# Score bursts of two pairs, an early Exp table, one maximum per head and a halved last output group in a two-layer encoder

## The chip, the cores and the metric

The kernel runs on one core of one Trainium2 chip. The metric is the device time of one execution in microseconds (us); lower is better. A core has five engines that run side by side and meet through semaphores: TensorE (PE in the profile; PEld are its weight loads), VectorE (DVE), ScalarE (ACT), GpSimd (POOL) and SyncE (SP), which issues most transfers. Matmul results land in PSUM, eight banks of 512 fp32 columns on 128 partitions.

## The reference, cut to what matters

Two layers of an encoder over 256 tokens of width 1024, in fp32. Each layer is a mixer and a channel sublayer:

```
h = rms_norm(x, n1);  proj = h @ w_in                  # 1024 -> 2560
a: 4 heads, neighbourhood attention with a bias        # q, k normed
d: 6 heads, dilated windows, q and k normed and rotated
c: 6 heads over 2 key heads, full attention, q and k normed and rotated
mix = [rms_norm(a), rms_norm(d), rms_norm(c)] * og;  x = x + mix @ w_out
h = rms_norm(x, n2);  g, u = split(h @ w_gate_up)      # 1024 -> 2 x 2816
g = conv3(g) + b;  x = x + (gelu(g) * u) @ w_down      # 2816 -> 1024
```

Every head's softmax is p = exp(s - max) / sum over 256 keys. With 256 tokens a head's scores are two token tiles of 128 rows and 256 columns, and one PSUM bank holds both.

## The kernel before, in words

**Arithmetic.** Each fp32 operand is split in a high part (a cast, on ScalarE) and a low part (operand minus high part, on VectorE), and a product is three matmuls: high x high, high x low, low x high (`mm3`, line 695). Weights arrive as raw tiles (4 buffers) through SyncE's queue and are split into hi and lo tiles (2 buffers of each) a unit at a time (`load`, `split`, `unit`, lines 640 to 693). Six units of layer 1's output projection are split while layer 0's feed-forward part runs, stored to DRAM (`keep`, line 624) and read back through GpSimd's queue.

**Stages of a layer.** Norm and transposes of x (`split_T`), projections into the four banks of the pool psa, then attention in the order d, c, a, with the projections and output projections woven in as filler (`Weave`), then `out_projections`, then the feed-forward part in eleven steps of 256 columns: gate G (`gate`, line 1373), U (`up`, line 1392), and down projection D (`down`, line 1402) in the order of `FFN` (line 77). The D of the last two steps come together, in four groups: two halves of 512 output columns by two token tiles. Lines 1437 to 1444 add each group to x on VectorE and, in the last layer, store it.

**Attention.** `scores(i)` (line 1210) computes two heads' scores in one burst of 12 matmuls of half height: the heads of a pair sit on partitions 0 to 63 and 64 to 127 and their matmuls run side by side. `softens` (line 1062) takes the row maximum (for d and a heads in one VectorE pass with the bias, for c heads by `reduce_max`), then Exp with its row sum on ScalarE, then the division. `turn` transposes the weights on TensorE and splits them, `weigh` multiplies them with the values. Scores, turned weights, transposed q and k, and the heads' outputs share the pool psw, four banks.

**Order.** All engines' order is planned before anything is emitted (`Plan`, line 238). Each operation has a rank, its number in program order plus shifts (`later`, `PLACES`). `order` (line 319) walks through time with a cost for each operation (`cost`, line 473) and always takes what can start earliest, lowest rank first. PSUM and SBUF buffers are given out strictly in program order of first use. A burst (`together`) runs without anything else between on TensorE, and starts only when all the buffers that it wants are free at once (`at_of_burst`, line 362). For transfers the planner books a rate and a latency (lines 436 to 448), and `LANDS` says when the thirteen first transfers land. The order is then fixed: on the chip each engine runs its list in order and waits by semaphore. `not_before(e)` makes an operation wait for the last one of engine e that was added so far.

The profile gives nearly every instruction line 470, where operations are emitted, so tiles tell them apart: `psw_w` and `psa_a` are the two PSUM pools, `wp_raw`, `wp_hi`, `wp_lo` weights, `act_ch` and `act_cl` the split turned weights in attention and the split product of gate and U in the feed-forward part, `act_s2k` scratch, `const_x` the running x, `small_nm` the negated maxima.

Of the kernel before, what the change touches and what calls it, by code (L numbers as in the profile page):

```python
# [11 lines left out]
F32 = mybir.dt.float32  # L12
# [6 lines left out]
P = 128  # L19
S = 256  # L20
# [31 lines left out]
LANDS = (4074, 3054, 5167, 3987, 5363, 6065, 7002, 7704, 8406, 9342, 10278, 10308, 10337)  # L52
# [172 lines left out]
def handover(a, b):  # L225
# [12 lines left out]
class Plan:  # L238
    def __init__(self, tc):
        self.tc, self.ops, self.shift, self.burst, self.bursts, self.behind = tc, [], 0, None, {}, None  # L240
        for name, short in (("tensor", "PE"), ("scalar", "ACT"), ("vector", "DVE"), ("gpsimd", "POOL"), ("sync", "SP")):
            setattr(self, name, PlanEngine(self, short, getattr(tc.nc, name)))
# [26 lines left out]
    def add(self, engine, method, args, kw):  # L269
# [16 lines left out]
        o.ns, o.lat, o.size, o.kind = cost(engine.name, method, args, kw, ins)  # L286
        o.before, o.after, o.first, o.tiles = set(), [], [], []
# [31 lines left out]
    def order(self):  # L319
# [79 lines left out]
        while len(done) < len(ops):  # L399
            best = None  # L400
            for e, r in ready.items():
                for i in r:
# [9 lines left out]
                    if at is not None and (best is None or (at, o.rank) < best[:2]):  # L412
                        best = (at, o.rank, i)
# [22 lines left out]
            if o.method == "dma_start":  # L436
# [6 lines left out]
                if e == "POOL":  # L443
                    end += 1000
                wires[ring] = end + shared / 120 + (o.size - shared) / (280 if i < self.first_loads else 335)
                end = wires[ring] + 1200
# [26 lines left out]
def cost(engine, method, args, kw, ins):  # L473

    out = args[0]
    if method == "dma_start":
# [3 lines left out]
        size = 4 * math.prod(w.shape) * (2 if small else 2 if spread else 1)  # L480
# [34 lines left out]
def encoder_kernel(  # L515
# [74 lines left out]
    nc.gpsimd.memset(minus_half, -0.5)  # L590

# [283 lines left out]
    for l in range(DEPTH):  # L875
# [181 lines left out]
        class Head:  # L1057
# [4 lines left out]
            def softens(self, sps):  # L1062
# [17 lines left out]
                else:  # L1080

                    for t in range(NT):
                        nc.vector.reduce_max(nm[:, t : t + 1], sps[t], axis=AX.X, negate=True)
# [125 lines left out]

        def scores(i):  # L1210

            two = heads[i : i + 2]
            sps = [psw.tile([P, NT, S], F32, tag="w", name=f"s_{z.name}") for z in two]
            g = two[0].group
            with nc.together():
                for t in range(NT):
                    for x, y in ((0, 0), (0, 1), (1, 0)):
                        for z, sp, rows_ in zip(two, sps, (LOW, HIGH)):
                            nc.tensor.matmul(
                                sp[:, t], turned[g + "q"][x][rows_, z.h // 2, t * P : (t + 1) * P],  # L1220
                                turned[g + "k"][y][rows_, z.kv if g == "c" else z.h // 2],
                                start=(x, y) == (0, 0), stop=(x, y) == (1, 0),
                            )
            for z, sp in zip(two, sps):
                z.softens([sp[:, t] for t in range(NT)])
# [147 lines left out]
        def gate(s):  # L1373
# [16 lines left out]
            made[s] = B  # L1390

# [10 lines left out]
        def down(steps):  # L1402
            ws = [unit() for _ in steps]
            for h in range(2):
                hs = slice(h * 512, (h + 1) * 512)
                for t in range(NT):
                    c = slice(t * P, (t + 1) * P)
                    for s, (wh, wl) in zip(steps, ws):
                        ch, cl = ready[s]
                        for j in range(2):  # L1410
                            mm3(
# [103 lines left out]
```

## Time and profile before

| | |
|---|---|
| median of three runs | 614.18 us (614.12 to 614.36) |
| profiled execution | 614.38 us, of which the span of instructions is 612.6 |
| TensorE busy | 604.5 us, 99% of the span, 3484 matmuls |
| VectorE, ScalarE busy | 485.4 us (79%), 428.5 us (70%) |
| GpSimd busy | 84.3 us (14%) |
| DMA | 121.44 MB, mean 198 GB/s |

A group row of the profile reads: line, engine, operation, out<-in, shapes, count, then busy us, mean ns of one, and the engine's idle time before it with what ended it. A timeline row reads: start in us, length in us, engine, instruction, and in brackets the idle time before it and its releaser. A row of a stretch reads: from:to, its length, then busy us with instruction counts in brackets for PE, PEld, DVE, ACT and POOL, the granted clock, the DMA engines' share and GB/s. Matmuls are pipelined: one's length reaches into the next, so what a matmul costs TensorE is the time from its start to the next one's.

### The profile page before, as it was taken

How to read it: one execution, taken by the hardware profiler on the slowest of the kernel's cores; microseconds unless marked ns; L12 is line 12 of the kernel's file. 1: busy time of each engine (PE TensorE's matmuls, PEld its weight loads, DVE VectorE, ACT ScalarE, POOL GpSimd, SP SyncE). 2: the span in 40 equal slices, each digit the busy share in tenths (PEclk: the TensorE clock that was granted, in tenths of full speed). 3: DMA queues.
4: the chain of work that ended last, by engine and by line, in shares of the span. 5: the costliest groups of instructions: out<-in, count | busy, mean ns of one | idle time of the engine just before them, and what ended most of it. 6: DMA issues, size and time to landing. Idle time of an engine off the chain costs nothing.

```text
span 612.6 us, 9883 instructions
## 1 busy us (share of the span) xinstructions
PE 604.5 (99%) x3484; PEld 525.2 (86%) x3484; DVE 485.4 (79%) x1000; ACT 428.5 (70%) x1064; POOL 84.3 (14%) x136
## 2 busy tenths in 40 slices
PE   8999999999999999999999999998999999999997
PEld 6998888888888888888899989887888888888885
DVE  4899989797788988887777788767877777777774
ACT  6789999696565766675588889857755656566661
POOL 2732130202400000000032214231000000000000
PEclk9999999999999999999999999999999999999999
DMA  8893403557589799987555626654665555556501
GB/s 272 294 294 141 139 25 105 184 159 242 166 225 326 247 360 326 349 293 251 155 155 182 215 70 240 206 178 129 202 217 179 175 197 201 167 185 205 189 18 68
DMA packets 85073, 121.44 MB, mean 198 GB/s; under 512 B 9864, under 2 KB 69608, under 8 KB 85024
## 3 DMA queue, kind: packets, MB, share of 16 engines
q1 hardware_dynamic: 82752, 112.17, 56.6%
q0 software_dynamic: 1728, 8.39, 4.0%
q8 instruction: 27, 0.44, 0.3%
q10 hardware_dynamic: 544, 0.26, 0.2%
q14 instruction: 22, 0.18, 0.1%
HBM read 110.93 MB, written 9.88 MB: 197 GB/s over the span
## 4 chain that ended last, share of the span: by engine, by line
PE 92%; DVE 2%; ACT 2%; POOL 1%; DMA 1%; issue 1%; SPq 0%; DVEq 0%; POOLq 0%
PE psw_w L470 51%; PE psa_a L470 41%; DMA const_x<-in_x_dram 1%; ACT act_s2k L470 1%; POOL small_rstd L470 1%; DVE const_x L470 1%; DVE wp_lo L470 1%; SPq L470 0%; DVE act_sw L470 0%; DVE act_z L470 0%; ACT wp_hi L470 0%; POOL small_ms L470 0%; ACT L470 0%; ACT act_z L470 0%; ACT act_hT L470 0%
## 5 line engine op out<-in xcount | busy, mean ns | idle before, releaser
L470 DVE TENSOR_TENSOR wp_lo<-wp_raw,wp_hi 128x512 fp32r<-128x512 f32 (+2 forms) x332 | 232.1, 735 | 53.9 <-ACT wp_hi L470 36.8
L470 ACT CAST wp_hi<-wp_raw 128x512 fp32r<-128x512 f32 (+2 forms) x332 | 202.5, 663 | 21.7 <-PE psa_a L470 9.1
L470 PE MATMUL psw_w<-act_hT,wp_hi 128*128 128x512 f32 x704 | 181.4, 393 | 0.0
L470 PEld LDWEIGHTS psw_w<-act_hT,wp_hi 128*128 128x128 f32 x704 | 128.1, 189 | 24.7
L470 PE MATMUL psa_a<-wp_hi,act_hT 128*128 128x384 f32 (+2 forms) x448 | 113.3, 332 | 0.5 <-ACT wp_hi L470 0.5
L470 PEld LDWEIGHTS psw_w<-act_hT,wp_lo 128*128 128x128 f32 x704 | 97.9, 190 | 6.9
L470 PE MATMUL psw_w<-act_hT,wp_lo 128*128 128x256 f32 x704 | 102.8, 282 | 0.0
L470 PEld LDWEIGHTS psa_a<-wp_hi,act_hT 128*128 128x128 f32 x448 | 78.1, 189 | 4.0 <-ACT wp_hi L470 0.8
L470 PE MATMUL psa_a<-wp_lo,act_hT 128*128 128x384 f32 (+2 forms) x224 | 74.2, 333 | 0.3 <-DVE wp_lo L470 0.2
L470 ACT COPY act_s2k<-psw_w 128x256 f32<-128x256 f32 x88 | 32.2, 371 | 58.7 <-PE psw_w L470 58.5
L470 PE MATMUL psa_a<-wp_lo,act_ch 128*128 128x512 f32 x176 | 69.4, 394 | 0.0
L470 PE MATMUL psa_a<-wp_hi,act_cl 128*128 128x512 f32 x176 | 69.4, 395 | 0.0
L470 PE MATMUL psa_a<-wp_hi,act_ch 128*128 128x512 f32 x176 | 68.9, 394 | 0.0
L470 DVE TENSOR_TENSOR act_s2k<-psw_w,act_s2k 128x256 f32<-128x256 f32 x88 | 36.7, 422 | 15.2 <-ACT act_s2k L470 14.9
L470 PEld LDWEIGHTS psa_a<-wp_lo,act_hT 128*128 128x128 f32 x224 | 42.2, 188 | 3.0 <-DVE wp_lo L470 1.7
L470 PEld LDWEIGHTS psa_a<-wp_hi,act_cl 128*128 128x128 f32 x176 | 33.2, 188 | 7.9 <-DVE act_cl L470 0.3
L470 PEld LDWEIGHTS psa_a<-wp_hi,act_ch 128*128 128x128 f32 x176 | 33.2, 189 | 6.7
L470 PEld LDWEIGHTS psa_a<-wp_lo,act_ch 128*128 128x128 f32 x176 | 33.1, 188 | 6.8
L470 DVE SCALAR_TENSOR_TENSOR act_s2k<-act_s2k,act_cw,act_s2k 128x255 f32<-128x255 f32 x88 | 36.8, 482 | 1.4 <-ACT act_s2k L470 1.3
L470 ACT ACTIVATE act_s2k<-act_s2k,act_cw 128x256 f32<-128x256 f32 x44 | 24.1, 595 | 18.0 <-DVE act_s2k L470 18.0
L470 ACT ACTIVATE act_s2k<-act_s2k 128x512 f32<-128x512 f32 x22 | 13.9, 631 | 30.0 <-DVE act_s2k L470 30.0
L470 POOL TENSOR_TENSOR small_rstd<-small_ms,const_mh 128x6 f32<-128x6 f32 (+2 forms) x26 | 31.7, 1218 | 2.2
(112 smaller groups left out, 794.7 us busy)
## 6 DMA issues: line engine op xcount, KB each, us to landing
wp_raw<-in_w_gate_up_dram SPq DMA_DIRECT2D x44, 1024.0 KB, 5.2
wp_raw<-in_w_down_dram SPq DMA_DIRECT2D x22, 1024.0 KB, 5.0
wp_raw<-in_w_in_dram SPq DMA_DIRECT2D x14, 768.0 KB, 6.3
wp_raw<-in_w_in_dram SPq DMA_DIRECT2D x8, 1024.0 KB, 8.8
wp_raw<-in_w_out_dram SPq DMA_DIRECT2D x8, 768.0 KB, 9.5
dram_khi<-act_mixT_hi SPq DMA_DIRECT2D x4, 768.0 KB, 9.5
dram_klo<-act_mixT_lo SPq DMA_DIRECT2D x4, 768.0 KB, 9.8
wp_lo<-dram_klo POOLq DMA_DIRECT2D x4, 768.0 KB, 5.4
```

The lines of the kernel that those rows point to most:

```text
L470: getattr(o.engine.real, o.method)(*map(real, o.args), **{k: real(v) for k, v in o.kw.items()})
```

## The change

- **Bursts.** `BURSTS` gives the number of pairs in a burst: heads d0 to d3 in one, d4 and d5 in one, c0 to c3, c4 and c5, a0 to a3. Each is one `together` over up to four score tiles; the softmax of the second pair is still added at its own place in the program.
- **Table.** Behind layer 0's last Gelu stands an Exp of one column into a new tile `few_out`, not before that Gelu in time. The planner's cost now has 1290 ns for each change between Exp and Gelu.
- **Maximum.** A c head's two token tiles have one `reduce_max` over the whole bank, two results wide.
- **Last group.** In the last layer, the down projection's last group (columns 512 to 1023 of the second token tile) is made in two halves of 256 columns, the second in a psw bank named `end`; each half has its own addition to x and its own store.
- **Planner.** Transfers: 360 bytes per ns in place of 335, 1000 ns latency in place of 1200, no further 1000 ns for GpSimd's queue, stores counted at 1.5 times their size; a tie goes to the lower number; new `LANDS` and `PLACES`. START and the warm-up, the order and number of first transfers, stay as they are.

```diff
--- before.py
+++ after.py
@@ -49,7 +49,7 @@
 ]
 
 
-LANDS = (4074, 3054, 5167, 3987, 5363, 6065, 7002, 7704, 8406, 9342, 10278, 10308, 10337)
+LANDS = (4100, 3300, 5300, 3450, 5800, 6450, 7250, 8200, 8900, 9800, 10700, 10750, 10800)
 
 
 WARM, WARM_MORE, WARM_W = 13, 15, 256
@@ -227,17 +227,18 @@
 
 
 PLACES = {
...
 }
 
 
 class Plan:
     def __init__(self, tc):
-        self.tc, self.ops, self.shift, self.burst, self.bursts, self.behind = tc, [], 0, None, {}, None
+        self.tc, self.ops, self.shift, self.burst, self.bursts, self.behind, self.table = tc, [], 0, None, {}, None, AF.Exp
         for name, short in (("tensor", "PE"), ("scalar", "ACT"), ("vector", "DVE"), ("gpsimd", "POOL"), ("sync", "SP")):
             setattr(self, name, PlanEngine(self, short, getattr(tc.nc, name)))
 
@@ -284,6 +285,9 @@
         if method == "matmul" and not kw["start"]:
             ins.append(args[0])
         o.ns, o.lat, o.size, o.kind = cost(engine.name, method, args, kw, ins)
+        func = args[2] if method == "activation" else None
+        if func in (AF.Exp, AF.Gelu) and func != self.table:
+            self.table, o.ns, o.lat = func, o.ns + 1290, o.lat + 1290
         o.before, o.after, o.first, o.tiles = set(), [], [], []
         for v in ins + outs:
             t = v.tile
@@ -409,7 +413,7 @@
                         at = at_of_burst(o.burst) if i == self.bursts[o.burst][0] else None
                     else:
                         at = at_of(o)
-                    if at is not None and (best is None or (at, o.rank) < best[:2]):
+                    if at is not None and (best is None or (at, o.rank, i) < best):
                         best = (at, o.rank, i)
             at, _, i = best
             o = ops[i]
@@ -440,10 +444,8 @@
                 shared = 0.0
                 if i < self.first_loads:
                     shared = o.size if ring == "ACT" else min(o.size, 120 * max(0.0, wires.get("ACT", 0.0) - end))
-                if e == "POOL":
-                    end += 1000
-                wires[ring] = end + shared / 120 + (o.size - shared) / (280 if i < self.first_loads else 335)
-                end = wires[ring] + 1200
+                wires[ring] = end + shared / 120 + (o.size - shared) / (280 if i < self.first_loads else 360)
+                end = wires[ring] + 1000
                 if i < self.first_loads:
                     end = LANDS[sum(p.method == "dma_start" for p in ops[:i])]
             for t in o.tiles:
@@ -477,7 +479,8 @@
         w = out if isinstance(out, View) else args[1]
         small = min(out.shape[-1], args[1].shape[-1]) < 128
         spread = isinstance(args[1], bass.AP) and args[1].ap[0][0] == 0
-        size = 4 * math.prod(w.shape) * (2 if small else 2 if spread else 1)
+        stored = isinstance(out, View) and out.tile.pool.dram
+        size = 4 * math.prod(w.shape) * (2 if small or spread else 1.5 if stored else 1)
         return 620 if engine == "POOL" else 480, 0, size, None
     n = out.width()
     psum = any(v.tile.pool.psum for v in ins)
@@ -588,6 +591,7 @@
 
     minus_half = const.tile([P, 32], F32, tag="mh", name="minus_half")
     nc.gpsimd.memset(minus_half, -0.5)
+    few_out = const.tile([P, 1], F32, tag="fo", name="few_out")
 
 
     vown, vkv = (
@@ -1059,7 +1063,7 @@
                 self.group, self.h, self.kv, self.bias, self.v = group, h, kv, bias, v
                 self.name = f"{group}{l}{h}"
 
-            def softens(self, sps):
+            def softens(self, sps, whole):
 
                 name, bias = self.name, self.bias
                 self.p = p = act.tile([P, NT, S], F32, tag="s2k", name=f"p_{name}", bufs=NS2K)
@@ -1079,8 +1083,7 @@
                         )
                 else:
 
-                    for t in range(NT):
-                        nc.vector.reduce_max(nm[:, t : t + 1], sps[t], axis=AX.X, negate=True)
+                    nc.vector.reduce_max(nm, whole, axis=AX.X, negate=True)
                     for t in range(NT):
                         nc.scalar.activation(
                             p[:, t], sps[t], AF.Exp, bias=nm[:, t : t + 1], accum_out=rs[:, t : t + 1]
@@ -1207,22 +1210,28 @@
             flat = nabs[l].rearrange("p r c -> p (r c)")
             return [flat[:, (h * RPB_ROWS + 3 - 2 * t) * GRID_W :][:, :S] for t in range(NT)]
 
+        BURSTS = {0: 2, 4: 1, 6: 2, 10: 1, 12: 2}
+        scored = {}
+
         def scores(i):
 
-            two = heads[i : i + 2]
-            sps = [psw.tile([P, NT, S], F32, tag="w", name=f"s_{z.name}") for z in two]
-            g = two[0].group
-            with nc.together():
-                for t in range(NT):
-                    for x, y in ((0, 0), (0, 1), (1, 0)):
-                        for z, sp, rows_ in zip(two, sps, (LOW, HIGH)):
-                            nc.tensor.matmul(
-                                sp[:, t], turned[g + "q"][x][rows_, z.h // 2, t * P : (t + 1) * P],
-                                turned[g + "k"][y][rows_, z.kv if g == "c" else z.h // 2],
-                                start=(x, y) == (0, 0), stop=(x, y) == (1, 0),
-                            )
-            for z, sp in zip(two, sps):
-                z.softens([sp[:, t] for t in range(NT)])
+            if i in BURSTS:
+                with nc.together():
+                    for n in range(i, i + 2 * BURSTS[i], 2):
+                        two = heads[n : n + 2]
+                        sps = [psw.tile([P, NT, S], F32, tag="w", name=f"s_{z.name}") for z in two]
+                        scored[n] = sps
+                        g = two[0].group
+                        for t in range(NT):
+                            for x, y in ((0, 0), (0, 1), (1, 0)):
+                                for z, sp, rows_ in zip(two, sps, (LOW, HIGH)):
+                                    nc.tensor.matmul(
+                                        sp[:, t], turned[g + "q"][x][rows_, z.h // 2, t * P : (t + 1) * P],
+                                        turned[g + "k"][y][rows_, z.kv if g == "c" else z.h // 2],
+                                        start=(x, y) == (0, 0), stop=(x, y) == (1, 0),
+                                    )
+            for z, sp in zip(heads[i : i + 2], scored[i]):
+                z.softens([sp[:, t] for t in range(NT)], sp)
 
         heads = []
         for h in range(H_DIL):
@@ -1388,6 +1397,9 @@
             B = act.tile([P, 2, S], F32, tag="s2k", name=f"B{nm}", bufs=NS2K)
             nc.scalar.activation(B, A, AF.Gelu)
             made[s] = B
+            if s == STEPS - 1 and l + 1 < DEPTH:
+                with nc.not_before("ACT"):
+                    nc.scalar.activation(few_out, minus_half[:, :1], AF.Exp)
 
         def up(s):
             nm = f"{l}_{s}"
@@ -1405,13 +1417,21 @@
                 hs = slice(h * 512, (h + 1) * 512)
                 for t in range(NT):
                     c = slice(t * P, (t + 1) * P)
-                    for s, (wh, wl) in zip(steps, ws):
-                        ch, cl = ready[s]
-                        for j in range(2):
-                            mm3(
-                                dacc[t][h], ch[:, j, c], cl[:, j, c], wh[:, j, hs], wl[:, j, hs],
-                                s == 0 and j == 0, s == STEPS - 1 and j == 1,
-                            )
+                    halved = l == DEPTH - 1 and steps[-1] == STEPS - 1 and (h, t) == (1, 1)
+                    if halved:
+                        end = psw.tile([P, S], F32, tag="w", name="end")
+                    for a, b in ((512, 768), (768, 1024)) if halved else ((hs.start, hs.stop),):
+                        for s, (wh, wl) in zip(steps, ws):
+                            ch, cl = ready[s]
+                            for j in range(2):
+                                apart = a == 768
+                                mm3(
+                                    end if apart else dacc[t][h][:, : b - a],
+                                    ch[:, j, c], cl[:, j, c], wh[:, j, a:b], wl[:, j, a:b],
+                                    (s == 0 or apart and s == steps[0]) and j == 0, s == STEPS - 1 and j == 1,
+                                )
+                    if halved:
+                        hold["end"] = end
 
         last = []
         NA_STEPS = {2: na_load, 3: na_repeat, 4: na_diagonals}
@@ -1440,8 +1460,15 @@
                 nc.vector.scalar_tensor_tensor(
                     xs[:, t, hs], dacc[t][h], r2[:, t : t + 1], xs[:, t, hs], ALU.mult, ALU.add
                 )
-                if l == DEPTH - 1:
-                    nc.sync.dma_start(ov[:, t, hs], xs[:, t, hs])
+                if l < DEPTH - 1:
+                    continue
+                if (h, t) == (1, 1):
+                    hs = slice(512, 768)
+                nc.sync.dma_start(ov[:, t, hs], xs[:, t, hs])
+        if l == DEPTH - 1:
+            hs = slice(768, 1024)
+            nc.vector.scalar_tensor_tensor(xs[:, 1, hs], hold["end"], r2[:, 1:2], xs[:, 1, hs], ALU.mult, ALU.add)
+            nc.sync.dma_start(ov[:, 1, hs], xs[:, 1, hs])
     nc.emit()
```

11 rows, old and new, of the table PLACES are left out of this document.

## The prediction

> **What bounds the kernel now.** I read the page's table of busy time first, then the stretches, then the chain.
>
> ```profile
> PE 604.5 (99%) x3484; PEld 525.2 (86%) x3484; DVE 485.4 (79%) x1000; ACT 428.5 (70%) x1064; POOL 84.3 (14%) x136
> ...
> 80.00:122.00 42.00, 41.93 (x274) 35.45 (x274) 37.49 (x91) 35.71 (x100) 10.37 (x14) 1.00 0.35 114
> 340.00:352.00 12.00, 11.50 (x84) 10.74 (x84) 8.41 (x27) 10.84 (x44) 3.19 (x4) 1.00 0.63 212
> 352.00:424.00 72.00, 70.44 (x479) 61.09 (x479) 55.29 (x153) 55.45 (x158) 19.23 (x31) 1.00 0.48 162
> 608.00:612.60 4.60, 0.60 (x3) 0.16 (x1) 0.75 (x1) 0.00 (x0) 0.00 (x0) 1.00 0.30 114
> ...
> 140.21 5.58 PE psa_a L470 x24
> ```
>
> TensorE is busy for 604.5 of 612.6 us at full granted clock (the 1.00 in the stretches). In the feed-forward part, 24 matmuls of 512 columns take 5.58 us in the chain, 0.2325 us each, without a pause. Nothing of the change removes columns there, so that part stays. Only four places can give time: TensorE's losses between matmuls in the attention parts, its idle at 340 to 352 (0.50 us), its idle at 352 to 424 (1.56 us), and the tail after 608, where 4.0 of 4.6 us have no matmul. ScalarE and VectorE matter where they run late: ScalarE is 90% busy at 340 to 352, VectorE 89% at 80 to 122.
>
> **Part 1, the bursts.** The timeline around the first score burst of layer 1; columns are start, length, instruction.
>
> ```profile
> 344.16 0.33 PE L470 MATMUL psa_a<-wp_lo,act_hT 128*128 128x384 f32 x1
> 344.33 0.34 PE L470 MATMUL psa_a<-wp_hi,act_hT 128*128 128x384 f32 x1
> 344.60 0.98 PE L470 MATMUL psw_w<-act_ko,act_qo 64*128 64x256 f32 x12
> 345.51 0.39 PE L470 MATMUL psa_a<-wp_hi,act_hT 128*128 128x256 f32 x1
> 345.73 0.28 PE L470 MATMUL psa_a<-wp_lo,act_hT 128*128 128x256 f32 x1
> 345.85 0.40 PE L470 MATMUL psa_a<-wp_hi,act_hT 128*128 128x256 f32 x2
> ```
>
> Matmuls overlap, so I price them from start to start. 384 columns cost 0.17 (344.16 to 344.33), 256 cost 0.12 (345.73 to 345.85). From 344.33 to 345.73 stand one of 384, twelve half-height ones running as six pairs of 256, and one of 256: 0.17 + 6 x 0.12 + 0.12 = 1.01. It took 1.40. So entering and leaving half-height mode costs 0.39 us. There are 8 bursts in a layer (16 heads in pairs); with BURSTS there are 5. The matmuls stay; 3 x 2 = 6 switches in and out go: 6 x 0.39 = 2.3, and since some bursts are followed by transposes rather than matmuls I take **-2.2 us**. TensorE has no idle time there to swallow it.
>
> What it adds is a claim on PSUM. The psw pool has 4 banks, given out in program order, and a double burst needs all four at once (at_of_burst). For the d heads that is free: their q and k have just been read out of PSUM when the scores may start. For c and a heads it isn't. Layer 1's first c and a bursts:
>
> ```profile
> 370.00 0.60 PE L470 MATMUL psw_w<-const_ident,act_s2k 128*128 128x128 f32 x4
> 372.27 0.97 PE L470 MATMUL psw_w<-act_kc,act_qc 64*128 64x256 f32 x12
> 372.59 0.70 DVE L470 TENSOR_TENSOR act_cl<-psw_w,act_ch 128x512 fp32r<-128x512 f32 x1
> ...
> 392.60 1.21 PE L470 MATMUL psw_w<-act_ko,act_qo 64*128 64x256 f32 x12
> 393.74 0.55 PE L470 MATMUL psw_w<-const_ident,act_s2k 128*128 128x128 f32 x3
> 394.04 0.47 PE L470 MATMUL psa_a<-wp_lo,act_mixT_hi 128*128 128x512 f32 x1
> 398.25 1.29 DVE L470 TENSOR_TENSOR act_cl<-psw_w,act_ch 128x512 fp32r<-128x512 f32 x2 [0.89 <-ACT act_ch L470]
> ```
>
> The turned weights written at 370.00 hold a bank until 373.29, 1.0 us past that burst. Those of 392.40 to 394.29 hold theirs to about 398.9, 6.3 us past the a burst, but only because ScalarE and VectorE took the first a pair's softmax first; that pair will not be there, and read at once (0.60 and 0.70 us, as the rows of such casts and VectorE's 372.59 show) the bank is free near 395.6, 3.0 us late. Behind the waiting burst TensorE can still run projections, which live in the other pool psa: matmuls of 512 columns start at 394.04 and fill that stretch today. Bounds for all four such bursts: 0 if covered, 2 x (1.0 + 6.3) = 14.6 if not covered at all; below 0 too, since the scores of the second pair come earlier. I take **+0.7**, near the covered end, because the busy row of 80 to 122 (41.93 of 42.00) shows that TensorE finds other work at every bank wait of today.
>
> **Part 2, the table.**
>
> ```profile
> 346.57 1.28 ACT L470 ACT_TABLE_LOAD   x1
> 347.86 0.51 ACT L470 ACTIVATE act_s2k<-act_s2k,small_nm 128x256 f32<-128x256 f32 x1
> 350.45 0.33 PE L470 MATMUL psw_w<-const_ident,act_s2k 128*128 128x128 f32 x1 [0.50 <-ACT act_s2k L470]
> ...
> 296.38 0.39 PE L470 MATMUL psa_a<-wp_hi,act_ch 128*128 128x512 f32 x1
> 296.72 2.36 DVE L470 TENSOR_TENSOR wp_lo<-wp_raw,wp_hi 128x1024 fp32r<-128x1024 f32 x2
> 297.30 0.62 ACT L470 ACTIVATE act_s2k<-act_s2k 128x512 f32<-128x512 f32 x1
> 297.83 0.62 ACT L470 COPY act_s2k<-psw_w 128x256 f32<-128x256 f32 x2
> 298.99 0.75 DVE L470 TENSOR_TENSOR act_s2k<-psw_w,act_s2k 128x256 f32<-128x256 f32 x2
> 300.50 0.62 ACT L470 CAST act_ch<-act_s2k 128x512 fp32r<-128x512 f32 x1 [2.06 <-DVE act_s2k L470]
> ```
>
> Layer 1's first Exp waits 1.28 us for its table, and the transposes of its result leave TensorE idle for 0.50; with the restart I take 0.6 as an estimate. That goes: **-0.6**, ends 0 and -0.7. Next late would be ScalarE's other work there, but without the load it is busy for 10.84 - 1.28 = 9.56 of 12 us. The load moves behind the Gelu at 297.30, ahead of one of the two U copies (the one-element Exp that carries it costs at most half of their 0.62 more; it is in the worse end below). That copy ends near 299.7 instead of 298.45, but VectorE was on weight splits until 299.08, so its sums slip by about 0.4 only and act_ch is ready near 301.5 instead of 301.12. TensorE meanwhile has the 24 matmuls of step 9 of the down projection, which need only the step before: from 296.38 on 24 x 0.2325 = 5.58 us, to 301.96. So **0**, and +0.5 if the order puts the load ahead of both copies.
>
> The Trainium skill (ScalarE: Activation LUTs, What ACT_TABLE_LOAD costs) adds a drain of about 1.38 us to each load, 2.66 in all. The trace disagrees: Exp starts 0.01 us after the load ends. By the page the moved load would outlast the cover, see rival D.
>
> **Part 3, planner and order.** The diff changes what the planner believes of transfers, so the whole order changes, and one place in the trace shows a loss that comes from this belief:
>
> ```profile
> 412.12 0.53 POOL L470 DMA_DIRECT2D wp_lo<-dram_klo  x1 [3.61 <-PE psa_a L470]
> 412.64 0.54 POOL L470 DMA_DIRECT2D wp_hi<-dram_khi  x1
> 417.12 0.40 PE L470 MATMUL psa_a<-wp_hi,act_mixT_lo 128*128 128x512 f32 x1
> 418.85 0.44 PE L470 MATMUL psw_w<-const_ident,const_x 128*128 128x128 f32 x2 [1.33 <-DVE const_x L470]
> 420.14 0.48 PE L470 MATMUL psa_a<-wp_hi,act_mixT_hi 128*128 128x512 f32 x1
> ...
> wp_hi<-dram_khi POOLq DMA_DIRECT2D x2, 512.0 KB, 4.3
> ```
>
> TensorE idles 1.33 us before the transposes of x, while the last output projection's 12 matmuls (OUT_ORDER[5], from 420.14) could run. Their weights, issued at 412.12 and 412.64, land after 4.3 us, near 416.9. By lines 438 to 446 the old planner books them at 413.48 + 1.0 + 1.565, then + 1.0 + 1.565 + 1.2 = 419.8, so it holds them back; the new one at 413.48 + 1.456 + 1.456 + 1.0 = 417.4. They would then fill the gap: **-1.2**, as a little of the wait for x remains. Bounds: 0 (the gap stays) and -1.9 (with the pauses that follow). The new LANDS and PLACES shift the rest of the order; the opening issues the same transfers and warm-up, so I take 0 there, with ends of 0.5 either way.
>
> **Part 4, one maximum.**
>
> ```profile
> L470 DVE TENSOR_REDUCE small_nm<-psw_w 128x1 f32<-128x256 f32 x24 | 8.8, 419 | 0.3
> L470 DVE SCALAR_TENSOR_TENSOR act_mixT_lo<-psw_w,const_gains,act_mixT_hi 128x256 fp32r<-128x256 f32 x16 | 7.7, 481 | 2.9 <-ACT act_sqm L470 1.5 <-ACT act_mixT_hi L470 1.4
> ```
>
> Twelve of 512 columns take the place of 24 of 256. VectorE saves near 1 us in all off the bounding engine: **0**.
>
> **Part 5, the tail.**
>
> ```profile
> 608.20 0.40 PE L470 MATMUL psa_a<-wp_hi,act_cl 128*128 128x512 f32 x1
> 608.64 0.75 DVE L470 SCALAR_TENSOR_TENSOR const_x<-psa_a,small_rx,const_x 128x512 f32<-128x512 f32 x1 [1.11 <-PE psa_a L470]
> ...
> out_dram<-const_x SPq DMA_DIRECT2D x4, 256.0 KB, 2.0
> ```
>
> Twelve matmuls of 512 become 24 of 256: 12 x (0.24 - 0.2325), +0.1. The last VectorE step shrinks from 0.75 to 0.48 (the row of 256 columns above): -0.27. The last store halves; what part of its 2.0 us goes with its bytes no row tells, so between 0 and -1.0, and I take -0.3, nearer the end at which most of it is fixed. The first half's store is issued six matmuls earlier and lies beside them. Together -0.27 - 0.3 + 0.1, **-0.5**, ends -0.2 and -1.2.
>
> Sum: -2.2 + 0.7 - 0.6 - 1.2 - 0.5 = -3.8. The profiled execution took 614.38 (span 612.6 and 1.8 around it), 0.2 above the median of 614.18; both give 610.4 to 610.6, I say **610.5**.
>
> **The rivals.** B, slower: the double a bursts wait for a PSUM bank and TensorE has no projection ready, because its filler was used up at the c bursts. For it: VectorE's 89% and the bank held to 398.9. Against: the matmuls at 394.04. Two a bursts at the 3.0 us above are 6.0 in place of 0.7: 615.8. It decides from 4.5 us of uncovered wait on. The Trainium skill (TensorEngine Tiling (Array Packing), Gotcha 1: PSUM Pressure) also warns that row tiling raises the demand on PSUM; the bank rows agree.
>
> C: bursts and tail gain, but the new order keeps the gap at 417 and half the table's gain goes into the down projection: 610.5 + 1.2 + 0.3 = 612.0.
>
> D: the switch of table holds ScalarE twice as long as its row, 2.6 us. Then act_ch comes near 302.8, 0.9 after the cover ends: 611.4. The page on the table load says this.
>
> E: the edits do what they say but the new order gives it all back in small waits: 614.2.
>
> **Chances.** A (forecast) 0.50, C 0.15, D 0.04, so faster 0.69; E 0.12; B 0.19. A measurement of this kernel can tell 0.2%, 1.2 us, from no change. The range leaves out the upper part of B and the case where the gap closes wholly and nothing is added (2.2 + 0.6 + 1.9 + 0.6 = 5.3 off 614.2, 608.9): 608.9 to 615.0.
>
> **What would show it.** Right: 10 rows of score bursts, six with 24 matmuls; no table load near 346 but one near 298, no TensorE idle before the first transposes of weights; the 1.33 us before the x transposes gone or small; a last VectorE step of 256 columns. Wrong: TensorE idle after c or a bursts released by VectorE or ScalarE, or idle on wp_hi or wp_lo landings.

## The result and the profile after

The changed kernel takes **610.35 us** in the median of five runs (610.2 to 611.12), the kernel before 614.12 (613.95 to 614.36): a ratio of 0.9941, with a 95% interval of 0.9927 to 0.9956. It is faster by 3.8 us, 0.6%. The profiled execution took 611.12 with a span of 609.3, the longest of the five; before it was 614.38 and 612.6. So the two spans differ by 3.3 only, and stage lengths below add up to that.

The head of the profile after, then the stretches whose rows of before stand in the prediction (columns as there).

```profile
span 609.3 us, 9892 instructions
...
PE 600.6 (99%) x3496; PEld 525.2 (86%) x3496; DVE 484.9 (80%) x989; ACT 428.4 (70%) x1065; POOL 84.6 (14%) x136
```

```profile
80.00:122.00 42.00, 41.94 (x275) 36.06 (x274) 37.36 (x85) 35.22 (x94) 7.93 (x12) 1.00 0.39 127
340.00:352.00 12.00, 12.00 (x102) 11.48 (x101) 9.57 (x37) 10.72 (x50) 3.20 (x4) 1.00 0.50 164
352.00:424.00 72.00, 70.60 (x476) 61.10 (x475) 55.92 (x142) 55.88 (x159) 20.34 (x34) 1.00 0.49 168
```

TensorE's pause at 340 to 352 is gone (11.50 before, 12.00 now). At 352 to 424 it still idles for 1.40 us (before 1.56). The busy share is 99% as before, but in us TensorE is busy for 3.9 less (600.6 against 604.5), and its idle time grew from 8.1 to 8.7. So the gain is not idle time won back: the stretches that count as busy became shorter. A switch of mode, for instance, counts as busy: the rows of the burst below have no idle time in brackets. Where the gain lies shows in where each stage starts. The next table gives the start of the first matmul of each stage, read from the timelines.

| stage begins with | before | after | step of the difference |
|---|---|---|---|
| first projection | 6.72 | 7.50 | +0.78 |
| first score burst, layer 0 | 46.07 | 45.77 | -1.08 |
| gate, layer 0 | 122.15 | 120.94 | -0.91 |
| first projection, layer 1 | 309.47 | 307.37 | -0.89 |
| first score burst, layer 1 | 344.60 | 343.08 | +0.58 |
| gate, layer 1 | 423.00 | 419.65 | -1.83 |
| last matmul | 608.20 | 604.83 | -0.02 |
| end of the span | 612.615 | 609.316 | +0.07 |

Most of the gain comes from the two attention stages (-0.91 and -1.83); the tail gives nothing. The -0.89 and +0.58 between them belong together: six matmuls that stood in the first of these two stages start in the second now (988 and 210 in place of 994 and 204), and -0.31 is left.

The opening is the least certain part. In this execution the first weights landed late (ScalarE's first cast of them starts at 6.56, before at 5.24), and TensorE idled 1.30 us in front of the first projection. Three runs below that share this opening (experiments 1 to 3) start the first burst at 45.54, 45.34 and 44.92, where the kernel before has 46.07 and 45.97 (experiment 4). So the opening gave 0.3 here and up to 1.1 elsewhere, and this is a likely reason why the medians differ by more than the spans.

Four views of the trace say why the attention stages are shorter.

**Bursts.** TensorE's timeline at layer 1's first burst:

```profile
342.82 0.34 PE L472 MATMUL psa_a<-wp_hi,act_hT 128*128 128x384 f32 x1
...
343.08 1.70 PE L472 MATMUL psw_w<-act_ko,act_qo 64*128 64x256 f32 x24
...
344.71 0.39 PE L472 MATMUL psa_a<-wp_hi,act_hT 128*128 128x256 f32 x1
...
344.94 0.28 PE L472 MATMUL psa_a<-wp_lo,act_hT 128*128 128x256 f32 x1
```

One row now holds 24 half-height matmuls. From 342.82 to 344.94 stand columns for 0.17 + 12 x 0.12 + 0.12 = 1.73; it took 2.12. So there is one switch of 0.39 for two pairs, where before there were two. The kernel has ten such rows, six of them with 24. Behind none of the six does TensorE idle.

**Table.** ScalarE around layer 0's last Gelu, then layer 1's first Exp:

```profile
295.84 0.62 ACT L472 ACTIVATE act_s2k<-act_s2k 128x512 f32<-128x512 f32 x1
...
296.37 0.61 ACT L472 COPY act_s2k<-psw_w 128x256 f32<-128x256 f32 x2
...
297.00 1.28 ACT L472 ACT_TABLE_LOAD   x1
...
298.30 0.20 ACT L472 ACTIVATE const_fo<-const_mh 128x1 f32<-128x1 f32 x1
...
299.05 0.62 ACT L472 CAST act_ch<-act_s2k 128x512 fp32r<-128x512 f32 x1 [0.55 <-DVE act_s2k L472]
...
345.20 0.51 ACT L472 ACTIVATE act_s2k<-act_s2k,small_nm 128x256 f32<-128x256 f32 x1 [0.16 <-DVE small_nm L472]
```

Both copies of U run ahead of the load (entries 2835 and 2837 of PLACES name them), and the cast behind it waits for VectorE, not for the table. TensorE has no wait there.

**The gap before x's transposes** is still there. TensorE and the transfers that GpSimd issues:

```profile
414.42 0.40 PE L472 MATMUL psa_a<-wp_hi,act_mixT_lo 128*128 128x512 f32 x1
415.92 1.09 PE L472 MATMUL psw_w<-const_ident,const_x 128*128 128x128 f32 x8 [1.10 <-DVE const_x L472]
416.77 0.48 PE L472 MATMUL psa_a<-wp_hi,act_mixT_hi 128*128 128x512 f32 x1
```

```profile
411.15 0.57 POOL L472 DMA_DIRECT2D wp_lo<-dram_klo  x1
411.72 0.54 POOL L472 DMA_DIRECT2D wp_hi<-dram_khi  x1
```

1.33 us have become 1.10, and the last output projection still follows the transposes (416.77). Its weights are issued only 0.9 us earlier than before (411.72 against 412.64), while x is ready 2.9 earlier (415.92 against 418.85): at the 4.3 us from issue to landing that the profile lists, the weights come at about 416.0 by this estimate, with x. What did go is the second pause. Before, the transposes stopped once more for the next part of x:

```profile
419.51 0.88 PE L470 MATMUL psw_w<-const_ident,const_x 128*128 128x128 f32 x6 [0.22 <-DVE const_x L470]
```

After, all eight run in one go. From the last projection ahead of the transposes to the first behind them it was 3.02 us (417.12 to 420.14) and is 2.35 now (414.42 to 416.77), 0.67 less. A new, small pause stands earlier, at 398.39, where TensorE waits 0.26 us for the landing of wp_hi.

**Tail.** TensorE and VectorE at the end:

```profile
604.83 0.39 PE L472 MATMUL psa_a<-wp_hi,act_cl 128*128 128x512 f32 x1
605.03 0.48 DVE L472 SCALAR_TENSOR_TENSOR const_x<-psw_w,small_rx,const_x 128x256 f32<-128x256 f32 x1 [0.55 <-PE psw_w L472]
605.43 0.74 DVE L472 SCALAR_TENSOR_TENSOR const_x<-psa_a,small_rx,const_x 128x512 f32<-128x512 f32 x1
```

The halves exist (the 128x256 row), but they are not last. Entry 5600 of PLACES pushes one 512-wide matmul of another group behind them, so the last VectorE step is again 512 wide. From the last matmul to the end it takes 4.49 us, before 4.42.

### The profile page after: what moved, and what is told of

Same layout as the page of the kernel before. It is cut to its first block, busy times and chain, and to the rows that moved or that the text cites. A ratio compares the mean times of both kernels' runs of the same rounds, so it can differ in the third digit from the quotient of the medians.

```text
span 609.3 us, 9892 instructions
## 1 busy us (share of the span) xinstructions
PE 600.6 (99%) x3496; PEld 525.2 (86%) x3496; DVE 484.9 (80%) x989; ACT 428.4 (70%) x1065; POOL 84.6 (14%) x136
## 4 chain that ended last, share of the span: by engine, by line
PE 91%; POOL 2%; issue 2%; DMA 2%; ACT 1%; DVE 1%; SPq 0%; DVEq 0%; POOLq 0%
PE psw_w L472 50%; PE psa_a L472 41%; DMA wp_hi<-dram_khi 1%; POOL small_rstd L472 1%; DMA wp_raw<-in_w_in_dram 1%; ACT act_s2k L472 1%; POOL small_ms L472 0%; DVE const_x L472 0%; ACT act_hT L472 0%; POOL act_sck L472 0%; POOL act_scq L472 0%; ACT wp_hi L472 0%; SPq L472 0%; POOL const_gq L472 0%; POOL act_sqm L472 0%
## 5 line engine op out<-in xcount | busy, mean ns | idle before, releaser
L472 PE MATMUL psa_a<-wp_hi,act_cl 128*128 128x512 f32 (+1 forms) x176 | 68.8, 393 | 0.0
L472 PE MATMUL psa_a<-wp_lo,act_ch 128*128 128x512 f32 (+1 forms) x176 | 68.7, 392 | 0.0
L472 PE MATMUL psa_a<-wp_hi,act_ch 128*128 128x512 f32 (+1 forms) x176 | 68.3, 392 | 0.0
```

Source lines behind the costliest of these rows:

```text
L472: getattr(o.engine.real, o.method)(*map(real, o.args), **{k: real(v) for k, v in o.kw.items()})
```

## The experiments

The theory after these views: bursts give 2.2 at most, the table 0.6 to 0.8, the tail and the gap nothing, and the order does the rest. The rivals: that the order alone does it, and that the bursts give back in waits what they save.

There are two kinds of kernel. In the first (experiments 2 to 4), the list of operations of one kernel is held fixed and one thing is changed in it. In the others, the planner makes its order anew; in experiment 1 this changes only the very end. Medians of five to twelve runs are compared with before on the same chip (614.37, 614.31 and 614.29 in the three batches). Differences to 610.35 cross batches: beside it, before took 614.12, so they may be 0.2 too large. The runs of one kernel spread by 0.6 to 2.4 us, so stage lengths from the traces are read beside the medians.

**1. The last matmul, put back in its place.**

```diff
-    4098: -190, 4099: -190, 4100: -190, 4119: 15, 4143: -98, 4210: -29, 4211: -29, 5600: 146,
+    4098: -190, 4099: -190, 4100: -190, 4119: 15, 4143: -98, 4210: -29, 4211: -29,
```

> The changed kernel without one entry of PLACES (5600: 146); only the last stretch's order changes: the second last group's last matmul stands in its own group again, and the half group of 256 columns ends. In the changed kernel's profile the end comes 4.49 us after the last matmul's start, against 4.42 in the kernel before. Theory (halving works, the shifted matmul undid it): last VectorE step 0.48 in place of 0.74 and no other step queued ahead of it, last store 128 KB: 0.4 to 0.9 us less than the changed kernel, 609.4 to 610.0. Rival (the end is fixed cost after the last result): under 0.2 us less, 610.2 to 610.4.

Measured: 610.04 (609.87 to 611.19), ratio 0.9936 [0.9924, 0.9949], span 608.3. The end of TensorE and VectorE:

```profile
604.47 0.28 PE L472 MATMUL psw_w<-wp_hi,act_cl 128*128 128x256 f32 x1
604.78 0.48 DVE L472 SCALAR_TENSOR_TENSOR const_x<-psw_w,small_rx,const_x 128x256 f32<-128x256 f32 x1 [0.55 <-PE psw_w L472]
```

From 604.47 to the end at 608.257 it takes 3.79 us, 0.70 less than after and 0.63 less than before: 0.12 from the narrower matmul, 0.27 from VectorE's step (0.75 to 0.48), and 0.22 from the smaller store (from VectorE's end to the span's end 3.00, before 3.22). The median is lower by 0.3 only, within its uncertainty, and lies between the two ranges that were named. The halved group works as a mechanism, and one shift had switched it off.

**2. The table load back at the first Exp, order of after held.**

```diff
-            if s == STEPS - 1 and l + 1 < DEPTH:
-                with nc.not_before("ACT"):
-                    nc.scalar.activation(few_out, minus_half[:, :1], AF.Exp)
```

> The changed kernel with its order held as it is and only the one-column Exp taken out, so that the table is loaded before layer 1's first Exp. Theory (the forecast's term): TensorE idles before the transposes of the first weights of layer 1, plus 0.6 us, 610.9 to 611.1. Rival (four heads' scores are ready at once, so the load is hidden by other ScalarE work or the filler): no more than 0.1 us, 610.3 to 610.5. Second rival (ScalarE is full there, the whole 1.28 us shows, since TensorE's filler is used up): 611.6.

Measured: 611.22 (610.79 to 611.44), ratio 0.9949 [0.9935, 0.9962], 0.9 above after. ScalarE's and TensorE's timeline:

```profile
344.43 1.28 ACT L750 ACT_TABLE_LOAD   x1
345.73 0.51 ACT L750 ACTIVATE act_s2k<-act_s2k,small_nm 128x256 f32<-128x256 f32 x1
...
350.85 0.33 PE L750 MATMUL psw_w<-const_ident,act_s2k 128*128 128x128 f32 x1 [0.27 <-ACT act_s2k L750]
```

The pause before the first transposes is back, and layer 1's attention (first burst to gate) takes 77.36 in place of 76.57. From layer 0's gate to layer 1's first projection it takes 186.40 (after: 186.43). So the table is worth 0.8, and its new place costs nothing. The time lies 0.1 above the theory's range.

**3. Each double burst cut in two, order of after held.** One full-height matmul that stood nearby is moved between the two pairs of each of the six double bursts; in TensorE's list:

```diff
 burst, pair 1 (12 half-height matmuls)
+one 128x256 or 128x512 matmul, taken from behind the burst
 burst, pair 2 (12 half-height matmuls)
```

> The changed kernel with its order held, but for six matmuls: in each double burst the next full-height matmul is moved between the two pairs, so that TensorE leaves half-height mode once more and comes back, with no other engine's order changed. Theory (the forecast's price of 0.39 us for a switch in and out): 6 x 0.39 = 2.3 us more, 612.5 to 612.8. Rival (the price holds only at a burst's ends and is partly hidden inside): 6 x 0.2 = 1.2 us, 611.5. Rival (the gain came from the new order, not from switches): under 0.4 us, 610.4 to 610.7.

Measured: 611.58 (611.07 to 612.22), ratio 0.9958 [0.9946, 0.9971], 1.2 above after. TensorE at the burst shown above:

```profile
342.97 0.98 PE L750 MATMUL psw_w<-act_ko,act_qo 64*128 64x256 f32 x12
343.88 0.38 PE L750 MATMUL psa_a<-wp_hi,act_hT 128*128 128x256 f32 x1
344.19 0.97 PE L750 MATMUL psw_w<-act_ko,act_qo 64*128 64x256 f32 x12
345.10 0.39 PE L750 MATMUL psa_a<-wp_lo,act_hT 128*128 128x256 f32 x1
```

From 342.97 to 345.10 it is 2.13 with one matmul of 0.12 inside; the double burst took 1.63. So a cut costs 0.38 where it stands: the price was right, 2.3 for six. But layer 0's attention grows by 0.76 only (75.17 to 75.93) and layer 1's by 0.23 (76.57 to 76.80). The time is that of the first rival, but not for its reason, since the price is not smaller inside a burst. Where the rest went is not shown. The 0.26 us for wp_hi at 398.39 are not in the cut kernel, but they are not in experiment 1 either, and the wait for x (1.10) is the same in both.

**4. The gap filled in the kernel before, its order held.** Six matmuls of the last output projection go ahead of x's transposes; in TensorE's list:

```diff
+6 x matmul psa_a<-wp, act_mixT      (last output projection)
 8 x matmul psw_w<-const_ident,const_x  (transposes of x)
-6 x matmul psa_a<-wp, act_mixT
```

> The kernel before with its order held, but for six matmuls: half of the last output projection of layer 1 runs ahead of the transposes of x, in the 1.33 us idle near 417.5. Theory (its weights land near 417, only the planner's belief held it back): 1.0 to 1.4 us less than the kernel before, 612.7 to 613.1. Rival (the weights land later than their row says, or what follows waits for x all the same): no gain, 614.0 to 614.3; TensorE then idles on wp_hi or on act_hT instead.

Measured: 614.22 (613.82 to 614.5), ratio 0.9996 [0.9987, 1.0006]: nothing, as the rival said. The gap did fill and the gate starts 1.55 earlier, at 421.45. TensorE, then VectorE:

```profile
421.45 0.50 PE L748 MATMUL psw_w<-act_hT,wp_hi 128*128 128x512 f32 x1
...
423.29 0.44 PE L748 MATMUL psw_w<-const_ident,const_x 128*128 128x128 f32 x2 [0.53 <-DVE const_x L748]
423.94 0.76 PE L748 MATMUL psw_w<-const_ident,const_x 128*128 128x128 f32 x5 [0.22 <-DVE const_x L748]
```

```profile
417.79 1.41 DVE L748 SCALAR_TENSOR_TENSOR const_x<-psa_a,small_rstd,const_x 128x512 f32<-128x512 f32 x2 [0.96 <-POOL small_rstd L748]
419.12 1.88 DVE L748 TENSOR_TENSOR wp_lo<-wp_raw,wp_hi 128x512 fp32r<-128x512 f32 x3
420.92 1.66 DVE L748 SCALAR_TENSOR_TENSOR act_hT<-psw_w,const_gains,act_hT 128x256 fp32r<-128x256 f32 x4
422.49 1.40 DVE L748 SCALAR_TENSOR_TENSOR const_x<-psa_a,small_rstd,const_x 128x512 f32<-128x512 f32 x2
```

VectorE is back to back from 419.12: weight splits, the normed transposes, then the second half of x at 422.49. TensorE waits for it at 423.29 and 423.94, and the first down-projection matmul starts only 0.35 earlier (440.57 against 440.92), of which 0.18 was there already at layer 1's first burst (344.42 against 344.60). The pause was a wait for x, whose first half waits for GpSimd (0.96 at 417.79) and whose second half waits for VectorE's own queue. Work that is pulled into the pause only moves the wait, at least in this order of VectorE; one with the second half of x ahead of the splits was not tried.

**5. One pair in each burst, order planned anew.** PLACES is keyed by the number of an operation, so its entries were renumbered to keep naming the same operations.

```diff
-        BURSTS = {0: 2, 4: 1, 6: 2, 10: 1, 12: 2}
+        BURSTS = dict.fromkeys(range(0, 16, 2), 1)
```

> The changed kernel with every pair in a burst of its own (8 bursts in a layer), planned anew, each shift of PLACES kept on its own operation. Splitting the double bursts with the order held cost 1.2 us in place of 2.3: half was absorbed. Theory (a switch costs 0.38 us, half of it hidden by waits that were there anyway): plus 0.9 to 1.4 us on the changed kernel's 610.35, 611.2 to 611.8. The forecast's own terms (-2.2 + 0.7): 611.8 to 611.9. Rival (the claim on four PSUM banks costs what the switches save): 610.1 to 610.6. Rival (PLACES fit only the double bursts, any new order loses 2 us): 612.5 or more.

**6. The old transfer model, order planned anew**, with the PLACES of after.

```diff
-                wires[ring] = end + shared / 120 + (o.size - shared) / (280 if i < self.first_loads else 360)
-                end = wires[ring] + 1000
+                if e == "POOL":
+                    end += 1000
+                wires[ring] = end + shared / 120 + (o.size - shared) / (280 if i < self.first_loads else 335)
+                end = wires[ring] + 1200
...
-        size = 4 * math.prod(w.shape) * (2 if small or spread else 1.5 if stored else 1)
+        size = 4 * math.prod(w.shape) * (2 if small or spread else 1)
```

> The changed kernel with the transfer model of the kernel before (335 bytes per ns, 1200 ns, 1000 ns more for GpSimd's queue, stores at their size), planned anew; on the chip no transfer is different in itself, only the order. The forecast's term (the new model lets the last output projection start in time): plus 1.2 us, 611.5. Theory after filling that gap by hand gained 0.15: no gain from there, plus 0 to 0.5, 610.3 to 610.9. Rival (PLACES fit only one order): plus 2 us and more, with the loss in other stages.

Measured: 5 took 615.91 (615.47 to 617.63), ratio 1.0027 [1.0014, 1.0039]; 6 took 614.17 (613.15 to 615.58), ratio 0.9998 [0.9988, 1.0008]. Both are times that the rival named, shifts that fit one order only. Either undoing alone loses the whole gain or more, 5.6 and 3.8 us, which together is far more than there was to lose. One row of kernel 5 shows part of what went wrong:

```profile
102.07 0.40 PE L472 MATMUL psa_a<-wp_hi,act_mixT_lo 128*128 128x512 f32 x1
104.04 0.39 PE L472 MATMUL psw_w<-act_ch,const_v 128*128 128x256 f32 x1 [1.58 <-ACT act_ch L472]
```

It is a new wait of 1.58 us that neither kernel has: the shifts fit one order, and these edits make another. The wait is not all. Right behind it TensorE's granted clock, the third figure from the end in the row of a stretch, falls to half:

```profile
106.00:108.00 2.00, 2.00 (x12) 2.00 (x11) 1.45 (x3) 1.00 (x3) 1.32 (x2) 0.50 0.00 0
```

It is 0.75 at 104 to 106, 0.50 here, 0.90 at 108 to 110 and 1.00 again from 110 on. Layer 0's attention takes 80.25 in this trace, 5.1 more than in after, and wait and lower clock together stand in it. The profiled execution took 617.24, above the median. No other trace here shows a lower clock before its last matmul, though some have pauses of 1.10 to 1.33 us; that the wait caused it is not shown. So 5 and 6 don't price their edits, and the next two runs take the shifts away from both kernels.

**7 and 8. No shifts at all**, in the kernel after and in the one before.

```diff
-PLACES = {
...
-}
+PLACES = {}
```

> The changed kernel with an empty PLACES, planned anew: what its shifts by hand are worth. Theory (features give most of the gain, the shifts a little in both kernels): plus 0.5 to 2 us, 610.9 to 612.4, and the difference to the kernel before with an empty PLACES stays near 3.8. Rival (most of the gain is the search for shifts): 613 or more, and that difference shrinks under 2.

> The kernel before with an empty PLACES, planned anew. Theory (features give most of the gain): 614.6 to 616.2, 3 to 4.5 us above the changed kernel with an empty PLACES. Rival (shifts give most of the gain): within 2 us of it.

Measured: after without shifts 613.5 (613.02 to 614.67), ratio 0.9987 [0.9978, 0.9997]; before without shifts 617.7 (617.09 to 618.7), ratio 1.0055 [1.0038, 1.0072]. The shifts are worth about the same in both, 3.2 and 3.4. The new shifts are therefore not the gain; without them after leads by 4.2. Both times lie above the theory's ranges, and the first is one that the rival named, but the difference is what the theory said (near 3.8, 3 to 4.5) and not under the rival's 2.

**9 and 10. The edits of 5 and 6, without shifts**, against 613.5.

> The changed kernel without any entry in PLACES (alone: 613.5) and with one pair in each score burst. If the bursts are worth what the held order showed, 2.3 by price of which half arrives at the end, this takes 614.7. If the double burst gives more than its switches, because the earlier scores of the second pair spare waits (as 615.9 for single bursts with shifts fitted to another order might mean), it takes 616 or more. If the 5.6 of that other kernel came from ill-fitting shifts alone, it takes 613.5 to 615.

> The changed kernel without any entry in PLACES (alone: 613.5) and with the old rates and latencies of transfers in the planner. If the new transfer model makes a better order by itself, the part of the 4.2 that bursts (1.2) and table (0.8) leave is its own, and this takes 615.5 to 616. If the model is worth nothing by itself and the 3.8 of the kernel with the fitted shifts came from shifts that no longer fit, it takes 613.5 within 0.5.

Measured: single bursts 613.21 (612.53 to 614.41), ratio 0.9981 [0.9972, 0.999]; old transfer model 616.23 (615.46 to 616.78), ratio 1.003 [1.0018, 1.0042]. None of the three ranges named for 9 holds its time; the last (613.5 to 615) came nearest, and the bursts are worth nothing by themselves. For 10 the transfer model is worth 2.7 by itself, a little more than the 2.2 that was left for it (the named range ended at 616). The edit takes back rate, latency, GpSimd's extra and the size of stores together, so which of them counts is not shown.

Lengths of the stages in the traces tell where (us, from the first matmul named to the next):

| | attention, layer 0 (burst to gate) | attention, layer 1 | last matmul to end |
|---|---|---|---|
| before | 76.08 | 78.40 | 4.42 |
| after | 75.17 | 76.57 | 4.49 |
| 7: after, no shifts | 77.39 | 76.00 | 3.80 |
| 9: 7 with single bursts | 76.29 | 77.34 | 3.79 |
| 10: 7 with old transfers | 77.41 | 78.65 | 3.81 |

Double bursts save 1.34 in layer 1's attention and cost 1.10 in layer 0's, and another 0.6 behind layer 1's gate. In layer 0, kernel 7 waits where kernel 9 doesn't; TensorE in layer 0's a heads:

```profile
103.33 0.39 PE L465 MATMUL psa_a<-wp_hi,act_mixT_lo 128*128 128x512 f32 x1
104.01 0.39 PE L465 MATMUL psw_w<-act_ch,const_v 128*128 128x256 f32 x1 [0.28 <-ACT act_ch L465]
104.73 0.39 PE L465 MATMUL psw_w<-act_cl,const_v 128*128 128x256 f32 x1 [0.34 <-DVE act_cl L465]
```

Not a bank is missing here, but turned weights: by the releasers, ScalarE and VectorE are late with a head's split. That four heads' scores at once make them late is a likely reading, not shown by itself. The old transfer model costs 2.65 in layer 1's attention, of the 3.7 by which the spans of the two profiled executions differ. TensorE in kernel 10:

```profile
402.91 0.40 PE L467 MATMUL psa_a<-wp_hi,act_mixT_hi 128*128 128x512 f32 x1
403.79 0.39 PE L467 MATMUL psw_w<-act_cl,const_v 128*128 128x256 f32 x1 [0.49 <-DVE act_cl L467]
...
417.74 0.50 PE L467 MATMUL psa_a<-wp_hi,act_mixT_hi 128*128 128x512 f32 x1 [0.69 <-DMA wp_hi<-dram_khi]
```

A planner that books the kept weights as late places the output projections late: the first one starts 42.3 us behind the stage's first burst, in kernel 7 38.7. They are then missing as cover (403.79), and their buffers come free late, so GpSimd issues the fifth pair of weights late (wp_hi at 413.42, 66.9 us behind the first burst, in kernel 7 63.4) and they truly land late (417.74).

## Why the prediction was right, and which of its steps weren't

The time (610.5 against 610.35) and the sign were right. Of the five terms that were not 0, one was right (table), one was right in price and half in effect (switches), one came out at half its size and by another way (the gap), and two came out at nothing (the wait for banks, the tail). The order, which stood at 0 elsewhere, carried the rest.

- **Bursts, -2.2 and +0.7.** The price of 0.39 a switch is confirmed (0.39 in after, 0.38 in experiment 3). The net of -1.5 is near what the held order gives, 1.2 by medians and 1.0 by stages, but for another reason: no bank was waited for, and about half of the saving does not arrive. What does not hold is the sentence that TensorE has no idle time there to swallow it. With the order left to the planner the bursts are worth nothing (experiment 9). The Trainium skill (TensorEngine Tiling (Array Packing), Key Properties) says that changing the tiling mode drains TensorE, without a price; the runs show that a change costs time, 0.38 to 0.39 in and out.
- **Table, -0.6.** Right; experiment 2 gives 0.8. A better order came than the two that were weighed: both copies of U run ahead of the load, and the load costs nothing at its new place. The Trainium skill (ScalarE: Activation LUTs, What ACT_TABLE_LOAD costs) has a drain of 1.38 us on top of the load. Here the load starts 0.02 us after the copies end (296.37 + 0.61 to 297.00), the one-column Exp 0.02 after the load (297.00 + 1.28 to 298.30), and undoing the move costs 0.8, so the 2.66 of that page, rival D, is not seen.
- **The gap, -1.2.** This step failed. It held that the planner's late booking kept the projections out of the gap. They stayed out, and the gap stayed at 1.10; by the estimate above, the weights land when x is ready. Experiment 4 shows that filling it gains nothing in the order before, since VectorE then is late with the second half of x. The prediction took a wait in front of an idle engine for the bound without asking what that engine needs next. The 0.67 that did go there came from x's transposes, which run without the second pause and behind a first one that is 0.23 shorter.
- **Order elsewhere, 0.** Of the 3.3 by spans, 1.0 for the bursts and 0.8 for the table leave 1.5 to the order. 0.67 of it is at x's transposes, 0.30 is the opening, 0.31 lies between layer 0's gate and layer 1's first burst, and the rest is spread over the attention stages. The prediction named a likely cause, the booking of transfers, and sought its effect at one place. By experiment 10 it acts over the whole stage: layer 1's attention is longer there by 2.65 of 3.7, and in the fitted order of experiment 6 by 1.85 (78.42 against 76.57).
- **Tail, -0.5.** As a mechanism right, 0.63 in experiment 1. In the changed kernel it is 0, because a shift that the diff lists, and that the prediction did not trace to its operation, puts a 512-wide matmul last.
- **The opening, 0 with 0.5 either way.** The first projection began 0.78 later, behind a transfer that landed late, and the first burst 0.30 earlier; other runs with this opening start that burst up to 0.85 earlier still.
- **The rivals.** B did not come: no idle time behind a double burst. Its kin showed without the shifts, as 1.1 us more in layer 0's attention, with waits for turned weights in it. Of C, the gap did stay, but the table's gain was kept. D fell. E, that the new order gives all back, is what a change of this kernel does when the shifts no longer fit (experiments 5 and 6). One of the signs of being wrong came in small, the 0.26 us on wp_hi at 398.39.

So the sum came out well because errors cancelled, which is luck. The switches were taken 1.2 too high, the gap and the tail 0.5 each; against that stand 0.7 for banks that never made it wait, 0.2 too little for the table, and the order with the opening, about 0.9 by spans and more by medians, for which the sum had nothing.

What stays open: what the order gave is what the held experiments leave over. It was not measured alone in the fitted order, since experiment 6 can't hold that order. Of the 4.2 without shifts, 2.7 for the transfers, 0.8 for the table (measured in the fitted order), 0.6 for the tail and -0.3 for the bursts make 3.8; the rest is within the spread of the runs, and that such parts add up is an assumption. The single maximum was not tried alone.

## What to carry to other kernels

A saving on the bounding engine need not arrive whole at the end, even where that engine is 99% busy: ask of each stage what its next stage waits for, and price an idle gap by what the engine needs behind the gap, not by its length. In a kernel whose order comes from a planner, a belief about transfer times can be worth more than an edit of the work (2.7 against 0 to 1.2 here). Shifts fitted to one order make single edits look worse than they are, so price an edit with the order held, or with all shifts taken out, and say that the two can differ (the bursts: 1.2 and -0.3).

## What the runs showed of the hardware

A switch of TensorE from full height to half height and back costs 0.38 to 0.39 us for 12 matmuls and for 24 alike. With a last store of half the columns the end comes only 0.22 us sooner (3.00 against 3.22 from VectorE's last step to the end of the span). Behind a pause of 1.58 us in kernel 5 TensorE's granted clock was 0.75, 0.50 and 0.90 in three stretches of 2 us; it stayed at 1.00 around the 1.33 us pause of the kernel before.
